# Transposed S5 input projection with a DRAM ring, and a background placed behind the residual, in a two-layer trunk

## The chip, the cores and the metric

One core of one Trainium2 chip runs the whole kernel. The metric is device time in microseconds of one execution. Matmuls run on TensorE (PE), elementwise work on VectorE (DVE), ScalarE (ACT) and GpSimd (POOL); transfers are issued from the queue of SyncE (SP) or, where the code says so, from GpSimd's.

## The reference

The program is a trunk of two layers on one sequence of 1024 positions and 1024 channels, in fp32. Each layer has a mixer and an MLP, and each of the four is wrapped as

```
shift, scale, gate = silu(c) @ W_mod + b_mod
x <- LayerNorm(alpha * x + (1 + gate) * sublayer(x * (1 + scale) + shift))
```

Layer 0's mixer is multi-head latent attention, layer 1's is S5, a diagonal state-space layer:

```
u = h @ w_in                                     # 1024 x 1024
bu = einsum(u in 64 groups of 16 channels, B)    # 64 complex states for each group
x_t = a * x_(t-1) + bu_t                         # a scan over the positions
y = Re(C x) + d * u
g = gelu(y);  z = g * sigmoid(g @ w_glu + b_glu);  return z @ w_out
```

The MLP is `relu(h @ w1 + b1)**2 @ w2 + b2` with 4096 hidden channels.

## The kernel before

Every large product is done on operands split in a high and a low part (`split`, L73 to L75: ACT copies the high part, DVE or POOL subtracts for the low one), with three matmuls for each (`mm3`, L78 to L80: high·high, high·low, low·high). X is held as eight row blocks of 128 positions by 1024 channels. `to_hT` (L863) transposes a pair of row blocks on PE (L874), scales and shifts them on ACT (L877) and splits them (L880, L881); the result h has channels in partitions and positions along the free axis, in two halves of 512 positions.

A scheduler sorts each engine's instructions by a simulation of the program, and each engine works its list off in that order; a semaphore wait at the head of a list holds everything behind it. `issue_after` adds an order without a wait between engines. So a text order in the code is a wish, and the list of each engine is what counts.

**MLP.** `mlp` runs 32 blocks of hidden channels, two per round g. `load1` loads and splits a block of w1, `load2` a block of w2 (L1005 multiplies it by the gate first), `mm1` makes the hidden block for one half of the positions into a PSUM tile of pool "a1" (two tiles) and squares it (ACT L1026 to L1028, DVE L1029), `mm2` multiplies by w2, and `accumulate` adds to X on DVE (L829). The residual (`alpha * x` with gain and bias) is done on X by POOL (L885, L886) before the first accumulation. `tick`, called in `mm1` and `mm2`, runs steps of a generator `bg` at a rate `pace`: in MLP 0 these are the modulations of three later sublayers (loads L561, products L563 on POOL and L568 on DVE, transposes L588) and the parameters of S5; in MLP 1 `bg` is empty.

**S5.** When MLP 0 closes, `finish0` normalises a row block, writes it to `x_d` and, after each second one, calls `to_hT`. The projection `u_strip(qr, s)` makes strip s (128 positions) of a quarter of the channels: positions are rows, 256 channels are columns, 24 matmuls, and ACT copies the PSUM tile to U (L1347). There are 32 such strips. The layer then runs 16 `front(b)`, each on four groups of channels: it transposes U by four PE transposes (L1385) with an ACT copy (L1388), applies B (L1392, 16 matmuls on the chip), rotates and scans on DVE (L1401 to L1406) and rotates back (L1409, one half on POOL, one on DVE) into zz. `back(b)` (L1417 to L1419, 24 matmuls) makes y, ACT applies the gelu (L1424), and every second back transposes it (L1432). A back follows its front by two. Tables of each front come in one load `pt` (1.5 MB, four buffers) and one `tz` for each pair.

**GLU.** For 8 blocks of channels and two halves of the positions a product lands in a PSUM tile of "a1" (L1472 on), the sigmoid and the gate follow, and `split` stores zT.

## Time and profile before

| | us |
|---|---|
| median of three runs | 2356.4 (2353.73 to 2360.72) |
| profiled execution, its own time | 2353.56 |
| its span, first to last instruction | 2351.4 |
| mean granted TensorE clock | 0.978 |
| MLP 0, from its first residual to its last matmul | about 485 to 1239 |
| S5, to the first GLU matmul | about 1239 to 1440 |
| MLP 1, with its end | about 1620 to 2351 |

A row of the waits reads: the engine and the line that waited, the engine and tile it waited for, then the sum in us, how often, and the longest. A row of the windows reads: the stretch, its length, then busy time and number of instructions of PE, PE's weight loads, DVE, ACT and POOL, then the granted clock, the busy share of the DMA engines and GB/s. A row of the timeline reads: start, duration, engine, line, operation, and in brackets the idle time before it with what ended it. Matmul records overlap by their pipelining, so the spacing of their starts is the cost of one.

### The profile page before, as it was taken

The numbers are of one execution on the slowest core, as the hardware profiler recorded it, in microseconds if no ns is written. First come the engines' busy times: TensorE is split into PE (matmuls) and PEld (weight loads), VectorE is DVE, ScalarE is ACT, GpSimd is POOL, SyncE is SP. The second block draws the span as 40 slices with busy tenths as digits, with TensorE's granted clock in tenths as the row PEclk, the third lists the DMA queues.
The fourth block names the chain that finished last, engine by engine and source line by source line (L and its number), as shares of the span: only waits on it lengthen the run. The fifth ranks groups of instructions, "written<-read, shape, count | busy, mean of one in ns | idle before, by whom it ended". The sixth has DMA issues, their size and how long they took to land.

```text
span 2351.4 us, 29181 instructions
## 1 busy us (share of the span) xinstructions
PE 2241.3 (95%) x11039; PEld 1885.4 (80%) x11039; DVE 1420.1 (60%) x2473; ACT 831.6 (35%) x1399; POOL 626.5 (27%) x731
## 2 busy tenths in 40 slices
PE   7799998979999999999998998999999999999996
PEld 6678886867788788888888997878788888888885
DVE  8877786387777766676444445454744444444437
ACT  3477774442222323333235233324322222222321
POOL 5534767371000334333021212433500000000005
PEclk8899998989999999999999999999999999999998
DMA  7222224135453345446123554330211111111201
GB/s 257 62 62 61 85 99 170 32 111 167 150 163 113 96 110 144 127 116 158 51 81 144 162 167 157 108 99 28 72 54 45 45 59 40 54 54 36 63 27 72
DMA packets 191579, 229.44 MB, mean 98 GB/s; under 512 B 45361, under 2 KB 136764, under 8 KB 189390
## 3 DMA queue, kind: packets, MB, share of 16 engines
q1 hardware_dynamic: 186558, 214.98, 29.4%
q0 software_dynamic: 3840, 12.59, 1.7%
q8 instruction: 87, 1.43, 0.2%
q14 instruction: 54, 0.44, 0.1%
q10 hardware_dynamic: 1040, 0.00, 0.0%
HBM read 190.88 MB, written 34.54 MB: 96 GB/s over the span
## 4 chain that ended last, share of the span: by engine, by line
PE 48%; DVE 3%; DMA 2%; ACT 1%; issue 1%; SPq 0%; POOL 0%; DVEq 0%; ACTq 0%; POOLq 0%
PE a L78 8%; PE a L80 8%; PE a L79 8%; PE mm L78 7%; PE mm L79 7%; PE mm L80 7%; PE mm L1392 1%; DMA wor<-in_ssm_w_out_dram 1%; DMA pt<-prm_d 1%; DVE ct L75 1%; PE a L1419 0%; PE a L1418 0%; PE a L1417 0%; DVE wo L75 0%; DVE X L1518 0%
## 5 line engine op out<-in xcount | busy, mean ns | idle before, releaser
L829 DVE TENSOR_TENSOR X<-X,mm 128x512 f32<-128x512 f32 x478 | 322.6, 684 | 286.1 <-PE mm L80 282.2
L78 PE MATMUL mm<-pb 128*128 128x512 f32 x512 | 203.0, 397 | 5.8 <-DVE X L829 5.8
L78 PE MATMUL a<-hT,pb 128*128 128x512 f32 x496 | 195.6, 394 | 11.0 <-DVE pb L1029 10.7
L79 PE MATMUL mm<-pb 128*128 128x512 f32 x512 | 199.7, 390 | 0.0
L80 PE MATMUL mm<-pb 128*128 128x512 f32 x512 | 199.7, 390 | 0.0
L80 PE MATMUL mm<-ct 128*128 128x512 f32 x512 | 199.2, 389 | 0.0
L79 PE MATMUL mm<-ct 128*128 128x512 f32 x512 | 199.2, 389 | 0.0
L78 PE MATMUL mm<-ct 128*128 128x512 f32 x512 | 198.5, 390 | 0.0
L78 PE MATMUL a<-hT,ct 128*128 128x512 f32 x496 | 193.3, 390 | 3.3 <-DVE ct L1029 3.3
L1026 ACT ACTIVATE a<-a,vt 128x512 f32<-128x512 f32 x128 | 83.5, 652 | 314.5 <-PE a L80 314.3
L80 PE MATMUL a<-hT,pb 128*128 128x512 f32 x496 | 194.4, 392 | 0.0
L79 PE MATMUL a<-hT,pb 128*128 128x512 f32 x496 | 194.4, 392 | 0.0
L80 PE MATMUL a<-hT,ct 128*128 128x512 f32 x496 | 193.1, 389 | 0.0
L79 PE MATMUL a<-hT,ct 128*128 128x512 f32 x496 | 193.0, 389 | 0.0
L885 POOL TENSOR_TENSOR X<-X,rb 128x1024 f32<-128x1024 f32 x6 | 14.8, 2480 | 634.5 <-ACT X L861 634.5
L1005 DVE TENSOR_TENSOR w2r<-w2r,gffn 128x1024 f32<-128x1024 f32 x64 | 87.6, 1371 | 132.4 <-DMA w2r<-in_mlp_w_dram 132.3
L78 PEld LDWEIGHTS a<-hT,pb 128*128 128x128 f32 x496 | 94.0, 190 | 31.7 <-DVE pb L1029 12.4
L78 PEld LDWEIGHTS mm<-pb 128*128 128x128 f32 x512 | 96.2, 188 | 27.3 <-DVE X L829 7.5
L78 PEld LDWEIGHTS mm<-ct 128*128 128x128 f32 x512 | 95.9, 188 | 20.9 <-DVE X L829 0.6
L80 PEld LDWEIGHTS mm<-pb 128*128 128x128 f32 x512 | 96.1, 188 | 20.2
L79 PEld LDWEIGHTS mm<-ct 128*128 128x128 f32 x512 | 96.2, 188 | 20.0
L79 PEld LDWEIGHTS mm<-pb 128*128 128x128 f32 x512 | 96.2, 188 | 19.7 <-issue 0.7
(492 smaller groups left out, 5414.5 us busy)
## 6 DMA issues: line engine op xcount, KB each, us to landing
w1r<-in_mlp_w_dram SPq DMA_DIRECT2D x64, 512.0 KB, 4.1
w2r<-in_mlp_w_dram SPq DMA_DIRECT2D x64, 512.0 KB, 3.3
pt<-prm_d SPq DMA_DIRECT2D x16, 1536.0 KB, 7.2
mb<-in_mod_mix_w_dram SPq DMA_DIRECT2D x41, 256.0 KB, 2.6
prm_d<-cb SPq DMA_DIRECT2D x80, 128.0 KB, 2.4
wm<-in_mod_mix_w_dram SPq DMA_DIRECT2D x8, 1024.0 KB, 11.8
mb<-in_mod_ffn_w_dram POOLq DMA_DIRECT2D x32, 256.0 KB, 3.0
mb<-in_mod_ffn_w_dram SPq DMA_DIRECT2D x32, 256.0 KB, 3.0
```

Source lines behind the costliest of these rows:

```text
L75: (eng or V).tensor_tensor(lo, src, f32(hi), ALU.subtract)
L78: PE.matmul(ps, lh, rh, start=start, stop=False)
L79: PE.matmul(ps, lh, rl, start=False, stop=False)
L80: PE.matmul(ps, ll, rh, start=False, stop=stop)
L829: V.tensor_tensor(xh, xh, ps[h], ALU.add)
L885: P.tensor_tensor(X[t], X[t], ra, ALU.mult)
L1005: V.tensor_tensor(r, r, gate, ALU.mult)
L1026: S.activation(ps, ps, AF.Relu, bias=vt2[:, l * 32 + j:l * 32 + j + 1])
L1392: PE.matmul(pvv[i][:, g * 128:g * 128 + 128], pt[:, i, g], ug[:, g], start=True, stop=True)
```

## The change

1. **Projection, transposed.** For layer 1 `to_hT` stores the strips in reversed order (`rev`). `u_half(m, hf)` now makes 128 channels by 512 positions: the weights are stationary, h is moving, 24 matmuls with 512 columns, 16 halves. ACT copies a half into U (L1357). When both halves of a channel block m are there, SP writes the block to DRAM (`ud[m]`, 512 KB, L1359), and `ug_load(b)` reads it back as four groups by 16 channels × 8 strips in partitions, with four transfers of 64 KB on GpSimd's queue (L1364), into a ring of four entries in the free part of U. `ug_load(b + 2)` stands behind `front(b)` and the back of b − 2. The transposes of U and their copies go.
2. **Loads of the projection's weights** come as 8 of 512 KB, one for each m, instead of 16 of 256 KB.
3. **Background.** `tick` does nothing until g = 1; then every step is ordered behind the load of w1 for that round. `pace` of MLP 0 goes from 0.6 to 0.66.
4. **Residual** in halves of 512 channels: four POOL operations for each row block.
5. **GLU**: the second half of each block takes its PSUM tile from pool "mm" (four tiles).

The order on DVE at the start of MLP 0, where the first squared hidden blocks (L1029 before, L1039 now; pb<-a) and the first weights are made. Before:

```order
L1029 TENSOR_TENSOR pb<-a_5174,pb 128x512
L881 TENSOR_TENSOR hT<-mm,hT 128x2x256 x4
L1005 TENSOR_TENSOR w2r<-w2r,gffn 128x1024 x2
L75 TENSOR_TENSOR pb<-w2r,pb 128x1024 x2
L568 SCALAR_TENSOR_TENSOR mb<-mb,csT 128x512
L1216 MEMSET tC 128x16
L1005 TENSOR_TENSOR w2r<-w2r,gffn 128x1024
L1217 MEMSET tC 128x16
L568 SCALAR_TENSOR_TENSOR mb<-mb,csT 128x512 x2
L75 TENSOR_TENSOR pb<-w2r,pb 128x1024
L1029 TENSOR_TENSOR pb<-a_5207,pb 128x512
L568 SCALAR_TENSOR_TENSOR mb<-mb,csT 128x512
```

Now:

```order
L1039 TENSOR_TENSOR pb<-a_5145,pb 128x512
L884 TENSOR_TENSOR hT<-mm,hT 128x2x256 x4
L1011 TENSOR_TENSOR w2r<-w2r,gffn 128x1024 x2
L1039 TENSOR_TENSOR pb<-a_5174,pb 128x512
L75 TENSOR_TENSOR pb<-w2r,pb 128x1024
L1227 MEMSET tC 128x16
L1228 MEMSET tC 128x16
L75 TENSOR_TENSOR pb<-w2r,pb 128x1024
L1039 TENSOR_TENSOR pb<-a_5203,pb 128x512
L1011 TENSOR_TENSOR w2r<-w2r,gffn 128x1024
L75 TENSOR_TENSOR pb<-w1r,pb 128x1024
L829 TENSOR_TENSOR X<-X,mm 128x512
```

The products of the background (L568) are gone from this stretch; the first of them stands nine rows further on. The hidden block that stood behind the third w2 product (L1005) now stands ahead of it.

On PE in the tail of S5, behind the last projection matmul. L1392 (now L1405) is a front, L1417 to L1419 (now L1430 to L1432) a back, each back with its own PSUM tile a. Before, around the last but one front:

```order
L1419 MATMUL a_12639<-pt,zz 128x128
L1392 MATMUL mm<-pt 128x128 x8
L1417 MATMUL a_12712<-tz,pt 128x128
L1418 MATMUL a_12685<-pt,zz 128x128
L1419 MATMUL a_12685<-pt,zz 128x128
```

Now, around the same front:

```order
L1405 MATMUL mm<-U,pt 128x128 x8
L1430 MATMUL a_12141<-tz,U 128x128
L1430 MATMUL a_12205<-tz,U 128x128
L1431 MATMUL a_12141<-pt,zz 128x128
L1405 MATMUL mm<-U,pt 128x128 x8
L1432 MATMUL a_12141<-pt,zz 128x128
```

Before, the back of b = 12 (a_12639 in the first row) was complete when front 14 came, and fronts 12 and 13 with two backs stood between back 10 and it. Now front 14 (the second row of L1405) follows front 13 with only three back matmuls between them, and backs 11 to 14 stand behind it.

On POOL in the tail of S5, where the first half of each zz is made (L1408 and L1409, now L1421 and L1422). Before:

```order
L1409 TENSOR_TENSOR zz<-pt 128x4x127
L1408 MEMSET zz 128x4
L1409 TENSOR_TENSOR zz<-pt 128x4x127 x2
L1408 MEMSET zz 128x4
L1462 TENSOR_SCALAR r_12778<-r_12778 128x512
L1409 TENSOR_TENSOR zz<-pt 128x4x127
```

Now:

```order
L1364 DMA U<-ud_5046 128x1x128 x4
L1421 MEMSET zz 128x4 x2
L1364 DMA U<-ud_5046 128x1x128
L1422 TENSOR_TENSOR zz<-pt 128x4x127 x3
L1364 DMA U<-ud_5046 128x1x128 x3
L1422 TENSOR_TENSOR zz<-pt 128x4x127
```

The loads of the ring (L1364, here those of the last channel block, for fronts 14 and 15) now stand between the zz rows, as they do throughout S5; each waits for the back that frees its place in the ring, and the zz rows behind it on POOL wait with it.

The diff, whole:

```diff
--- before.py
+++ after.py
@@ -860,12 +860,15 @@
         E.tensor_scalar(nm, mu, rs, -1.0, ALU.mult, ALU.mult)
         S.activation(X[t], X[t], AF.Identity, bias=nm, scale=rs)
 
-    def to_hT(ts, n, A, tile=None):
+    def to_hT(ts, n, A, tile=None, rev=False):
 
         g = len(ts)
         m = 4 // g
-        hi, lo = A[ts[0] // 4]
-        c0 = (ts[0] % 4) * 128
+        p0 = ts[0]
+        if rev:
+            p0, ts = 7 - ts[-1], ts[::-1]
+        hi, lo = A[p0 // 4]
+        c0 = (p0 % 4) * 128
         for k0 in range(0, 8, m):
             ps = (tile or tr_tile)()
             for k in range(m):
@@ -882,8 +885,10 @@
         return last_.ins
 
     def residual(t, ra, rb):
-        P.tensor_tensor(X[t], X[t], ra, ALU.mult)
-        P.tensor_tensor(X[t], X[t], rb, ALU.add)
+        for r, op in ((ra, ALU.mult), (rb, ALU.add)):
+            for h in range(2):
+                sl = slice(h * 512, h * 512 + 512)
+                P.tensor_tensor(X[t][:, sl], X[t][:, sl], r[:, sl], op)
 
     def res_row(wp, v, al=ALPHA, gb2=None, name="rb"):
 
@@ -994,8 +999,9 @@
             if j >= NJ:
                 return
             r = wp.tile([128, 8, 128], F32, tag="wr", name="w1r")
-            SY.dma_start(r, w1r[j])
+            d = SY.dma_start(r, w1r[j])
             split(*w1_buf(j), r)
+            return d.ins
 
         def load2(j):
             if j >= NJ:
@@ -1007,11 +1013,15 @@
             return d.ins
 
         credit = [0.0]
+        behind = []
 
         def tick(w):
+            if not behind:
+                return
             credit[0] += w * pace
             while credit[0] >= 1.0:
-                step(bg)
+                with tc.issue_after(behind[0]):
+                    step(bg)
                 credit[0] -= 1.0
 
         def mm1(j, h):
@@ -1061,8 +1071,9 @@
             residual(t, ra, rb)
         for g in range(NJ // 2 - 2):
             j = 2 * g + 2
-            load1(j + 1)
+            d = load1(j + 1)
             if g:
+                behind.append(d)
                 mm1(j, 0)
             mm1(j, 1)
             load2(j)
@@ -1325,26 +1336,32 @@
 
     gTf = []
     kdr = kd.rearrange("g a f -> a g f")
-    wir = ssm_w_in[0].rearrange("(k p) f -> p k f", p=128)
+    wir = ssm_w_in[0].rearrange("(k p) (m f) -> m p k f", p=128, f=128)
+    ud = [drm.tile([128, 1024], F32, name=f"ud{m}") for m in range(8)]
     WI = {}
 
-    def u_load(qr):
-
-        WI[qr] = [xp.tile([128, 2, 2, 256], F32R, tag="X", name="wi") for _ in range(4)]
-        for i in range(4):
-            if i % 2 == 0:
-                r2 = wp.tile([128, 2, 2, 256], F32, name="wir", **(dict(tag="a4", bufs=1) if qr else dict(tag="wr")))
-            r = r2[:, i % 2]
-            SY.dma_start(r, wir[:, 2 * i:2 * i + 2, qr * 256:qr * 256 + 256])
-            split(WI[qr][i][:, :, 0], WI[qr][i][:, :, 1], r, V if qr else P)
-
-    def u_strip(qr, s):
-        ps = a1_tile()[:, 0:256]
+    def u_load(m):
+
+        r = wp.tile([128, 8, 128], F32, name="wir", **(dict(tag="wr") if m < 2 else dict(tag="a4", bufs=1)))
+        SY.dma_start(r, wir[m])
+        WI[m] = [xp.tile([128, 8, 128], F32R, tag="X", name="wi") for _ in range(2)]
+        split(*WI[m], r, P if m < 2 else V)
+
+    def u_half(m, hf):
+
+        ps = a1_tile() if hf and m < 3 else mm_half()
+        wh, wl = WI[m]
+        hh, hl = T5["h"][hf]
         for k in range(8):
-            hh, hl = [q[:, k, (s % 4) * 128:(s % 4) * 128 + 128] for q in T5["h"][s // 4]]
-            w_ = WI[qr][k // 2]
-            mm3(ps, hh, hl, w_[:, k % 2, 0], w_[:, k % 2, 1], k == 0, k == 7)
-        S.activation(U[:, qr % 2, :, 7 - s], ps.rearrange("p (g c) -> p g c", g=16), AF.Copy)
+            mm3(ps, wh[:, k], wl[:, k], hh[:, k], hl[:, k], k == 0, k == 7)
+        S.activation(U[:, m % 2, hf * 512:hf * 512 + 512], ps, AF.Copy)
+        if hf == 0:
+            SY.dma_start(ud[m], U[:, m % 2])
+
+    def ug_load(b):
+        us = ud[b // 2].rearrange("(g c) (s n) -> g s c n", c=16, s=8)
+        for g in range(4):
+            P.dma_start(UG[b % 4][:, g], us[(4 * b + g) % 8])
 
     def finish0(t, ps):
         accumulate(t, ps)
@@ -1355,17 +1372,19 @@
         norm(t)
         SY.dma_start(x_d[t], X[t])
         if t % 2:
-            to_hT((t - 1, t), 1, T5["h"], mm_half if t == 7 else None)
+            to_hT((t - 1, t), 1, T5["h"], mm_half if t == 7 else None, True)
         if t == 5:
             u_load(0)
-
-    mixer = mlp(0, hT, cont, gffn, wp, bg, finish0, w1x, rb, pace=0.6)
+            u_load(1)
+
+    mixer = mlp(0, hT, cont, gffn, wp, bg, finish0, w1x, rb, pace=0.66)
     next(mixer)
     mixer.send(o_end(7, ps))
     step(mixer, 100)
 
 
-    U = pa1.tile([128, 2, 16, 8, GC], F32, tag="pa", name="U")
+    U = pa1.tile([128, 4, 1024], F32, tag="pa", name="U")
+    UG = [U[:, 2 + i // 2, (i % 2) * 512:(i % 2) * 512 + 512].rearrange("p (g n) -> p g n", g=4) for i in range(4)]
     tzG = {}
 
     BK = {}
@@ -1379,13 +1398,7 @@
                 SY.dma_start(tz[16 * s:16 * s + 16], kdr[:, 4 * b:4 * b + 8, 16 * s:16 * s + 128])
             tzG[0] = tz
             tzG[1] = {}
-        ps = tr_tile()
-        for g in range(4):
-            gl = (4 * b + g) % 16
-            PE.transpose(ps[:, g * 128:g * 128 + 128],
-                         U[:, (b // 4) % 2, gl].rearrange("p s c -> p (s c)"), ident)
-        ug, w = pt[:, 6], pt[:, 7]
-        S.activation(ug.rearrange("p g n -> p (g n)"), ps, AF.Copy)
+        ug, w = UG[b % 4], pt[:, 7]
         pvv = mm_tile()
         for i in range(2):
             for g in range(4):
@@ -1432,19 +1445,23 @@
                     PE.transpose(ps[:, i * 128:i * 128 + 128], G[:, 4 * h + i], ident)
                 S.activation(gTf[k][:, h * 512:h * 512 + 512], ps, AF.Copy)
 
-    for s in range(8):
-        u_strip(0, s)
-    strips = {0: (1, 0, 2), 1: (1, 2, 4), 2: (1, 4, 6), 3: (1, 6, 8), 5: (2, 0, 2), 6: (2, 2, 5), 7: (2, 5, 8),
-              9: (3, 0, 2), 10: (3, 2, 5), 11: (3, 5, 8)}
+    u_load(2)
+    for hf in (1, 0):
+        for m in range(2):
+            u_half(m, hf)
+    for b in range(4):
+        ug_load(b)
     for b in range(16):
-        if b in (0, 3, 7):
-            u_load((0, 3, 7).index(b) + 1)
-        qr, s0, s1 = strips.get(b, (0, 0, 0))
-        for s in range(s0, s1):
-            u_strip(qr, s)
+        m = b // 2 + 2
+        if m < 8:
+            if b % 2 == 0 and m > 2:
+                u_load(m)
+            u_half(m, 1 - b % 2)
         front(b)
         while len(BK) > 2:
             back(min(BK))
+        if 2 <= b < 14:
+            ug_load(b + 2)
     while BK:
         back(min(BK))
     q = pa_tiles([128, 4, 1024], F32R, "gT")
@@ -1469,7 +1486,7 @@
         split(gh, gl, r)
         for hf in range(2):
             sl = slice(hf * 512, hf * 512 + 512)
-            ps = a1_tile()
+            ps = a1_tile() if hf == 0 else mm_half()
             for k in range(8):
                 mm3(ps, gh[:, k], gl[:, k], gTh[k][:, sl], gTl[k][:, sl], k == 0, k == 7)
             S.activation(ps, ps, AF.Sigmoid, bias=vt1[:, VGLU + m:VGLU + m + 1])
```

## Prediction

> **What bounds the kernel now.** I read the page first, the busy time of the engines.
>
> ```profile
> PE 2241.3 (95%) x11039; PEld 1885.4 (80%) x11039; DVE 1420.1 (60%) x2473; ACT 831.6 (35%) x1399; POOL 626.5 (27%) x731
> ```
>
> TensorE (PE) is busy 2241.3 of the span's 2351.4 us, so an edit can pay in two ways only: less work on PE, or less of its 110 us of idle time (and of the slow clock that follows idle time). So the second view is what PE waited for:
>
> ```profile
> PE a L78 <- DVE pb L1029: 10.7, 1, 10.7
> PE mm L78 <- DVE X L829: 7.5, 7, 1.9
> PE tr L874 <- DVE h L881: 4.2, 3, 1.7
> PE a L78 <- ACT U L1347: 3.5, 1, 3.5
> PE a L78 <- DVE zT L75: 3.4, 1, 3.4
> ```
>
> The longest single wait of the kernel stands first: 10.7 us at the start of MLP 0. The others lie at the entry of the S5 layer (L874, L1347) and at the first GLU tiles (zT); L829's seven are spread over both MLPs. The third view is stretches around the longest wait (busy time of PE, its weight loads, DVE, ACT and POOL; then the granted clock), the fourth the timeline of VectorE (DVE) there:
>
> ```profile
> 490.00:500.00 10.00, 7.71 (x32) 5.99 (x32) 8.54 (x10) 8.31 (x17) 10.00 (x5) 0.74 0.27 80
> ...
> 520.00:525.00 5.00, 0.00 (x0) 0.00 (x0) 4.98 (x2) 1.48 (x3) 5.00 (x3) 0.50 0.34 105
> 525.00:530.00 5.00, 3.33 (x8) 2.66 (x9) 5.00 (x4) 0.00 (x0) 5.00 (x2) 0.50 0.53 160
> 530.00:535.00 5.00, 5.00 (x19) 3.98 (x18) 5.00 (x4) 0.14 (x1) 4.36 (x2) 0.77 0.59 207
> ...
> sum 50.00, PE 36.99 PEld 29.53 DVE 46.28 ACT 18.68 POOL 44.36; mean PE 4.62 PEld 3.69 DVE 5.79 ACT 2.34 POOL 5.55
> ```
>
> ```profile
> 517.17 2.81 DVE L568 SCALAR_TENSOR_TENSOR mb<-mb,csT 128x512 f32<-128x512 f32 x1
> 522.66 3.35 DVE L75 TENSOR_TENSOR pb<-w2r,pb 128x1024 fp32r<-128x1024 f32 x1
> 525.94 0.68 DVE L1029 TENSOR_TENSOR pb<-a,pb 128x512 fp32r<-128x512 f32 x1
> 537.22 0.74 DVE L568 SCALAR_TENSOR_TENSOR mb<-mb,csT 128x512 f32<-128x512 f32 x1
> 539.68 1.22 DVE L75 TENSOR_TENSOR pb<-w1r,pb 128x1024 fp32r<-128x1024 f32 x1
> ```
>
> From 490 to 540 us PE idles 13.0 us (50.00 less 36.99), with the clock down to 0.50. DVE is full: background products (L568) and weight splits (L75) stand ahead of the L1029 that PE waits for, and while GpSimd (POOL) is full with the residual they take 2.81 and 3.35 us instead of 0.74 and 1.22.
>
> **Term A, entry of MLP 0: −12.** What is lost there now: 13.0 idle; the longest wait on L829, 1.9, which comes just after; and the busy time at a low clock, 7.71 × 0.26 + 3.33 × 0.50 + 5.00 × 0.23 = 4.8. Together 19.7 us. The change moves the background (its products, transposes and loads) behind g=1, so no L568 is left ahead of the first splits, and cuts each residual into halves. What stays can be read off MLP 1, the same code with an empty background:
>
> ```profile
> 700.00:730.00 30.00, 30.00 (x138) 24.95 (x137) 23.73 (x34) 9.40 (x13) 0.70 (x1) 1.00 0.55 176
> 1620.00:1650.00 30.00, 27.89 (x136) 22.99 (x135) 12.46 (x26) 19.97 (x37) 17.72 (x9) 0.97 0.15 53
> 1650.00:1680.00 30.00, 26.65 (x110) 20.73 (x109) 26.60 (x16) 11.09 (x16) 28.13 (x10) 0.97 0.26 88
> ```
>
> Idle 2.1 + 3.4, clock loss 60 × 0.03 = 1.8: 7.3 us. 19.7 − 7.3 = 12.4; I take 12, since one L563 that waits for a load still stands between the last residual halves. Bounds −8 (the 10.7 alone, of which one stretched operation, 2.8, stays) to −17 (nearly all of it). The background itself is not dearer: in 700–730 PE is full with DVE at 23.7 of 30, and its last transposes come 97 matmuls (22 us) later in PE's order, still ahead of the S5 layer. If that cover were gone, its 124 steps would end up on the S5 entry.
>
> **Term B, S5 work on PE: −12.2.**
>
> ```profile
> L78 PE MATMUL a<-wi,h 128*128 128x256 f32 x244 | 70.5, 290 | 3.5 <-ACT U L1347 3.5
> L1385 PE MATMUL tr<-ident,U 128*128 128x128 f32 x64 | 9.3, 273 | 0.0
> L1409 POOL TENSOR_TENSOR zz<-pt 128x508 f32<-128x508 f32 x16 | 27.3, 1704 | 137.6 <-DVE zz L1408 126.8 <-PE tr L1432 10.8
> ```
>
> Matmul records overlap, so I price by starts: 256 columns 0.12 us apart, 512 columns 0.226 apart:
>
> ```profile
> 1240.14 0.28 PE L78 MATMUL a<-wi,h 128*128 128x256 f32 x1
> 1240.26 0.28 PE L79 MATMUL a<-wi,h 128*128 128x256 f32 x1
> ...
> 1236.39 0.39 PE L78 MATMUL mm<-pb 128*128 128x512 f32 x1
> 1236.62 0.39 PE L79 MATMUL mm<-pb 128*128 128x512 f32 x1
> ```
>
> 768 × 0.12 = 92.2 becomes 384 × 0.2265 = 87.0: −5.2. The 64 transposes of U (L1385), 0.11 apart, go: −7.0. ScalarE's 16 copies after them go too; it has room. Bounds ±1.
>
> **Term C, S5 entry: +3 (−3 to +8).**
>
> ```profile
> 1250.00:1255.00 5.00, 2.04 (x16) 1.63 (x15) 2.68 (x4) 5.00 (x12) 0.07 (x1) 1.00 0.10 29
> 1255.00:1260.00 5.00, 1.38 (x7) 1.17 (x8) 3.28 (x6) 4.96 (x12) 0.00 (x0) 0.60 0.93 355
> ...
> L877 ACT ACTIVATE tr<-tr,bcol,acol 128x256 f32<-128x256 f32 x16 | 8.3, 568 | 5.2 <-PE tr L874 4.0 <-DVE bni L122 1.3
> L880 ACT ACTIVATE h<-tr 128x512 fp32r<-128x512 f32 x8 | 5.0, 656 | 0.0
> ```
>
> ScalarE's chain (scale, split of h) is full here and PE starves: 6.6 us. That chain keeps its length. But before, projection matmuls fill the gaps ahead of the last X transposes (26 of them, 3.1 us); in the changed order the transposes come first. In ScalarE's changed order 22 scalings (0.57), 9 splits (0.66) and two weight splits (about 1) stand between the last row block of X and the first copy of U: 20.5 us, so it comes near 1265. By then PE has done 46 wide matmuls (10.4 us) instead of some 120 narrow ones (14.4): 4 us behind. I take 3, as nothing later in the entry waits for ScalarE's U copies of a single strip (the 3.5 of L1347) any more. First front: after its half, 34 matmuls (7.7 us) stand ahead of it on PE; the trip takes 0.6 copy, 3.1 write, 0.6 issue, 2.9 load = 7.2, so it is just covered.
>
> ```profile
> x_d<-X SPq DMA_DIRECT2D x8, 512.0 KB, 3.1
> ...
> L561 POOL DMA_DIRECT2D mb<-in_mod_ffn_w_dram x32: 538/587/587, 142.6 to 309.5; - x32
> ...
> DMA to landing us min/median/max: 2.5/2.9/5.3
> ```
>
> In the steady part each front gets 4 GpSimd issues: 4 × 0.57 + 1.7 (its zz) = 4.0 us of about 10.4 per front (half 5.4, front 1.8, back 2.7, transposes 0.4). On POOL some zz stand behind an issue that waits for the back two fronts before; PE then has another back and transposes (3.8 us) in hand. Nothing to 0.5 each; in C's range.
>
> **Term D, S5 tail: +4 (0 to +10).** pt has four buffers, so pt(14) loads only when back(10) is done.
>
> ```profile
> 1400.69 1.79 PE mm L1392 x16
> 1409.06 12.61 DMA pt<-prm_d
> 1430.51 1.80 PE mm L1392 x16
> 1437.43 0.49 PE a L1419 x2
> ...
> pt<-prm_d SPq DMA_DIRECT2D x16, 1536.0 KB, 7.2
> ```
>
> Before, the last projection ends at T0 = 1400.5, pt(14) starts 8.5 us later, takes 12.6 (two at once), and front(14) follows at once; GLU begins at T0 + 39. Now PE does after T0 front(11) (1.8), eight transposes (0.9), front(12) (1.8) and back(10) (24 × 0.11 = 2.7): pt(14) can start at T0 + 7.2 and lands 7.2 later, or more. Front(14) follows right behind front(13), at T0 + 9.5: a stall of 5. The backs put behind it cover pt(15) but leave front(15) to its own chain of scans: 5.1 us (1430.51 + 1.8 to 1437.43). The tail ends near T0 + 38.5, though it holds 4.9 us less work (back(9), transposes); 2.7 of that was only moved before T0. So about 4 of B's gain is not seen.
>
> **Terms E, F, G.** E: the 3.4 us at zT comes of having two PSUM tiles for all sigmoid halves, so that the third half waits until the first is read out; now every second half takes a tile of another pool: −3.4 (−4 to 0, should that pool's tiles be held by the S5 tail). F: halves in MLP 1: −1 (−3 to +1). G, at the end:
>
> ```profile
> 2330.20 4.71 DVE L1518 SCALAR_TENSOR_TENSOR X<-X,bmv,rb 128x512 f32<-128x512 f32 x2
> 2342.70 1.40 DVE L1519 SCALAR_TENSOR_TENSOR X<-X,bny,rb 128x512 f32<-128x512 f32 x2
> ```
>
> The same form takes 2.36 beside POOL and 0.70 alone; halves let it in earlier: −2 (−4 to 0).
>
> **Sum.** −12 − 12.2 + 3 + 4 − 3.4 − 1 − 2 = −23.6, from the profiled execution's 2353.6 to 2330.0. The median shown is 2.8 above that execution, so I forecast 2332 for a median.
>
> **Rivals.** (1) The S5 gain goes to its seams: C at +8 and D at +10 cost 11 more: 2344. For it: two starved chains are touched; against: the ring looks ahead two fronts. (2) The MLP 0 wait was DVE beside POOL, not the background: splits still take 3.35, A is −4: 2341. For it: L75 is stretched without L568; against: MLP 1. (3) Slower: GpSimd's queue becomes the bound. Issues for b+4 wait for back(b), and a zz stands behind them, so back(b), 4 issues, zz and the next back form a loop: 4d + 1.7 + 2.7 against 10.4 per front. It binds from d = 1.5 us. If DVE stretches an issue as it is stretched itself (2.81/0.74 = 3.8, so d = 2.17), 13 fronts lose 2.7 each: 35 more, 2367; the whole gain is eaten from d = 2. Against it: the 32 issues in the attention part took 538 to 587 ns. (4) The change does not do what it says: the background returns in a burst behind g=1 and stalls L829 there, A −2: 2343.
>
> On rival 3, the Trainium skill, "SBUF — State Buffer" (A bandwidth-pool intuition that's wrong), states that a GpSimd-queued DMA of about 620 ns takes about 3100 ns beside a DVE copy, as its descriptors wait for the port. By that rule the loop would be 16.8 us, an estimate of 83 us lost in 13 fronts, and the kernel near 2415; no row here shows such an issue, and the 587 ns speak against it.
>
> **Chances.** Forecast 0.60, rival 1 0.18, rival 2 0.10, rival 3 0.07, rival 4 0.05. Range: the forecast's terms reach 2318 with A at −17 and the seams at their best halves; above, it takes in rivals 1, 2 and 4 to 2350. 0.3% (7 us) is what a measurement can tell from no change. The forecast and most of rivals 1, 2 and 4 are below 2349: faster 0.83; their upper ends same 0.09; rival 3 and mishaps of the seams slower 0.08.
>
> **What would show it.** A: no wait above 3 us on the L1039 that was L1029, and a clock near 1 in 510–540. B: no transposes of U, 384 matmuls 0.226 apart. C: PE waits between the last MLP matmul and the first front of 8 to 14 us in sum. D: one wait on pt for front(14), one on zz after front(15). E: no wait on zT. Rival 3: issues of L1364 above 1.5 us and PE waiting on zz in every front. The forecast is wrong if the S5 layer as a whole is not shorter, or if MLP 0's entry still loses over 13 us.

## The result and the profile after

The changed kernel takes 2382.6 us (median of 4 runs, 2378.8 to 2387.8) against 2356.8 for the kernel before: a ratio of 1.011 (95% interval 1.0084 to 1.0136). It is slower by 26 us where 24 us faster was forecast. The profiled execution took 2384.7 us, its span is 2383.0.

Where the time went, by the starts of the first and last matmuls of each stage in the two traces (us; the differences, each rounded by itself, add up to the difference of the spans, 31.6, within 0.1):

| stretch | before | after | difference |
|---|---|---|---|
| up to the first hidden block of MLP 0 (pb in L78) | 480.2 | 482.3 | +2.1 |
| from there to the last matmul of MLP 0 | 759.4 | 742.3 | −17.1 |
| S5 and GLU, to the last matmul of the GLU | 292.3 | 313.3 | +21.0 |
| output projection, to the first hidden block of MLP 1 | 93.1 | 93.7 | +0.7 |
| from there to MLP 1's first product with w2 | 29.7 | 49.9 | +20.2 |
| the rest of MLP 1 | 678.8 | 676.4 | −2.3 |
| from its last matmul to the end | 18.1 | 25.0 | +6.9 |

So the entry of MLP 0 gave more than was forecast, and three other places lost 48 us. The page of the changed kernel shows nearly the same busy time of TensorE, with 448 instructions fewer (64 transposes and 384 matmuls), over a longer span; the waits of TensorE show the new places:

```profile
PE 2242.5 (94%) x10591; PEld 1869.8 (78%) x10591; DVE 1416.1 (59%) x2467; ACT 819.7 (34%) x1359; POOL 666.3 (28%) x837
```

```profile
PE mm L78 <- ACT ct L74: 20.2, 1, 20.2
PE mm L1405 <- DMA pt<-prm_d: 11.4, 4, 3.9
...
PE mm L1405 <- DMA U<-ud: 5.1, 2, 4.5
PE tr L877 <- DVE h L884: 4.1, 1, 4.1
...
PE a L78 <- DVE pb L1039: 2.9, 3, 1.9
```

The 10.7 us on pb (L1029, now L1039) are down to 2.9 in three waits. On top stands a wait of 20.2 us that did not exist, in MLP 1, where the kernel's own code changed by nothing but the halves of the residual. The next two rows are S5's: fronts that wait for their tables (pt) and for the ring (ud).

**Entry of MLP 0.** The stretch in which TensorE was busy for 19.27 us of 30, before and after:

```profile
510.00:540.00 30.00, 19.27 (x74) 15.36 (x73) 27.74 (x21) 7.01 (x10) 24.36 (x9) 0.77 0.46 149
510.00:540.00 30.00, 27.98 (x116) 22.31 (x114) 19.14 (x19) 6.99 (x11) 27.66 (x19) 0.94 0.37 115
```

**Entry of MLP 1.** Before, the first two multiplications of w2 by the gate (L1005, now L1011) took 5.88 us beside whole residuals:

```profile
1650.94 5.88 DVE L1005 TENSOR_TENSOR w2r<-w2r,gffn 128x1024 f32<-128x1024 f32 x2
```

Now, in the timelines of VectorE, ScalarE, GpSimd and TensorE:

```profile
1657.65 23.91 DVE L1011 TENSOR_TENSOR w2r<-w2r,gffn 128x1024 f32<-128x1024 f32 x2
1681.48 0.68 DVE L1039 TENSOR_TENSOR ct<-a,ct 128x512 fp32r<-128x512 f32 x1
...
1680.46 2.19 ACT L74 ACTIVATE ct<-w2r 128x1024 fp32r<-128x1024 f32 x2 [23.07 <-DVE w2r L1011]
...
1654.78 11.16 POOL L891 TENSOR_TENSOR X<-X,rb 128x512 f32<-128x512 f32 x9
...
1674.40 4.94 POOL L891 TENSOR_TENSOR X<-X,rb 128x512 f32<-128x512 f32 x4
...
1681.57 2.07 PE L78 MATMUL mm<-ct 128*128 128x512 f32 x4 [20.18 <-ACT ct L74]
...
L1011 DVE TENSOR_TENSOR w2r<-w2r,gffn x4: 1211/1226/22776, 1657.7 to 1699.0; 128x1024 f32<-128x1024 f32 x4
```

The same two multiplications take 23.91 us; the last row (shortest, median and longest of the line's operations) tells that one of them took 22.8 us where the median is 1.2. It begins at 1657.7 and ends just after GpSimd's row of halves does: the row ends at 1674.40 + 4.94 = 1679.3, the operation at 1680.4, about its own length of 1.2 us later. GpSimd's halves meanwhile run through at 1.24 us each, as if alone. ScalarE waits for the product, TensorE for ScalarE. In MLP 0 of the same execution the same pair of operations beside the same halves took 3.94 us, and the halves gave way:

```profile
498.37 3.94 DVE L1011 TENSOR_TENSOR w2r<-w2r,gffn 128x1024 f32<-128x1024 f32 x2
...
487.72 17.97 POOL L891 TENSOR_TENSOR X<-X,ra 128x512 f32<-128x512 f32 x12
```

**The end.** The same once more, with the last layer norm's residual:

```profile
2354.80 13.41 DVE L1535 SCALAR_TENSOR_TENSOR X<-X,bmv,rb 128x512 f32<-128x512 f32 x2
...
2337.18 29.82 POOL L891 TENSOR_TENSOR X<-X,rb 128x512 f32<-128x512 f32 x24 [657.84 <-ACT X L861]
```

13.41 us for two operations that took 4.71 before; they end a little after GpSimd's 24 halves do (2367.0).

**S5.** TensorE's waits in its timeline, and what the loads cost:

```profile
1229.95 1.97 PE L877 MATMUL tr<-ident,X 128*128 128x128 f32 x8 [4.08 <-DVE h L884]
1276.32 1.22 PE L1405 MATMUL mm<-U,pt 128*128 128x128 f32 x4 [4.45 <-DMA U<-ud]
1315.38 0.98 PE L1405 MATMUL mm<-U,pt 128*128 128x128 f32 x3 [3.87 <-DMA pt<-prm_d]
1343.84 0.87 PE L1405 MATMUL mm<-U,pt 128*128 128x128 f32 x5 [2.83 <-DMA pt<-prm_d]
1389.18 0.57 PE L1405 MATMUL mm<-U,pt 128*128 128x128 f32 x3 [2.04 <-DMA pt<-prm_d]
1411.78 0.46 PE L1405 MATMUL mm<-U,pt 128*128 128x128 f32 x2 [2.62 <-DMA pt<-prm_d]
...
L1364 POOL DMA_DIRECT2D U<-ud x64: 582/622/762, 1272.9 to 1425.5; - x64
DMA to landing us min/median/max: 2.2/3.9/9.8
```

The issues on GpSimd are short (at most 0.76 us), so they are not stretched. Their landing takes 3.9 us in the median and up to 9.8. Three of the waits on pt lie ahead of the last projection matmul (1401), where before TensorE waited for nothing from the first front on, and two of them lie in stretches with a lower granted clock:

```profile
1310.00:1340.00 30.00, 26.13 (x163) 23.88 (x162) 12.26 (x23) 5.58 (x10) 11.32 (x17) 0.89 0.66 193
1340.00:1370.00 30.00, 27.17 (x157) 23.99 (x157) 14.47 (x29) 4.46 (x8) 8.32 (x14) 0.94 0.96 258
```

Cut at the same events, S5 before and after: from MLP 0's last matmul to the first front 48.8 and 51.7 us; from there to the last projection matmul 112.1 and 124.9; from there to the last transposes of the gelu 41.0 and 47.1. None of the 12.2 us of work that went is seen in these lengths. The rows of the whole stretch from MLP 0's last matmul to the GLU's, before and after, show what covers it:

```profile
1239.57:1531.83 292.26, 276.77 (x1969) 258.12 (x1968) 133.61 (x231) 104.76 (x182) 70.91 (x66) 0.98 0.44 146
1224.60:1537.90 313.30, 281.37 (x1530) 244.45 (x1528) 135.68 (x227) 96.15 (x150) 113.63 (x132) 0.93 0.53 163
```

TensorE's idle time grew from 15.5 to 31.9 us, and its clock went down: it stood at 0.50 for 10.2 us before and for 44.4 after, in nine pieces of 3.4 or 6.8 us. Five of these pieces begin within, or less than 1 us behind, a wait of 2.6 to 4.5 us in the timeline above. Multiplying busy time by the missing share of the clock, as the prediction did for MLP 0, but cut at each change of the clock, gives a loss of 3.5 us before and 19.0 after. What is left of the busy time, the work at full clock, is 273.3 and 262.3 us. By this estimate 11 us of work did go, and 16 us of new waits together with 16 us of slow clock hide it.

### The profile page after: what moved, and what is told of

The parts are those of the page before. It is cut to its first block, busy times and chain, and to the rows that moved or that the text cites. A ratio compares the mean times of both kernels' runs of the same rounds, so it can differ in the third digit from the quotient of the medians.

```text
span 2383.0 us, 28399 instructions
## 1 busy us (share of the span) xinstructions
PE 2242.5 (94%) x10591; PEld 1869.8 (78%) x10591; DVE 1416.1 (59%) x2467; ACT 819.7 (34%) x1359; POOL 666.3 (28%) x837
## 3 DMA queue, kind: packets, MB, share of 16 engines
q1 hardware_dynamic: 191678, 219.18, 29.7%
## 4 chain that ended last, share of the span: by engine, by line
PE 66%; DVE 6%; DMA 5%; POOL 3%; issue 2%; ACT 1%; SPq 1%; DVEq 0%; POOLq 0%; ACTq 0%
PE mm L78 12%; PE mm L80 12%; PE mm L79 12%; PE a L78 9%; PE a L80 9%; PE a L79 9%; POOL X L891 2%; DVE w2r L1011 1%; DMA pt<-prm_d 1%; DMA w2r<-in_mlp_w_dram 1%; PE mm L1405 1%; DVE X L1535 1%; DVE X L829 1%; DMA wor<-in_ssm_w_out_dram 1%; PE tr L877 0%
## 5 line engine op out<-in xcount | busy, mean ns | idle before, releaser
L891 POOL TENSOR_TENSOR X<-X,rb 128x512 f32<-128x512 f32 x56 | 75.1, 1386 | 657.8 <-ACT X L861 657.8
L78 PE MATMUL mm<-ct 128*128 128x512 f32 x512 | 199.2, 391 | 20.2 <-ACT ct L74 20.2
L78 PE MATMUL mm<-pb 128*128 128x512 f32 x512 | 201.9, 396 | 3.7 <-DVE X L829 3.5
L78 PE MATMUL a<-hT,pb 128*128 128x512 f32 x496 | 195.9, 395 | 2.9 <-DVE pb L1039 2.9
L78 PE MATMUL a<-hT,ct 128*128 128x512 f32 x496 | 193.5, 390 | 0.0
L1011 DVE TENSOR_TENSOR w2r<-w2r,gffn 128x1024 f32<-128x1024 f32 x64 | 105.5, 1651 | 133.1 <-DMA w2r<-in_mlp_w_dram 133.0
L78 PEld LDWEIGHTS mm<-ct 128*128 128x128 f32 x512 | 96.5, 189 | 40.7 <-ACT ct L74 20.6
L78 PEld LDWEIGHTS mm<-pb 128*128 128x128 f32 x512 | 96.4, 188 | 26.2 <-DVE X L829 5.4
L78 PEld LDWEIGHTS a<-hT,pb 128*128 128x128 f32 x496 | 93.6, 189 | 23.9 <-DVE pb L1039 4.2
L80 PEld LDWEIGHTS mm<-pb 128*128 128x128 f32 x512 | 96.4, 188 | 20.3
```

Source lines behind the costliest of these rows:

```text
L78: PE.matmul(ps, lh, rh, start=start, stop=False)
L80: PE.matmul(ps, ll, rh, start=False, stop=stop)
L891: P.tensor_tensor(X[t][:, sl], X[t][:, sl], r[:, sl], op)
L1011: V.tensor_tensor(r, r, gate, ALU.mult)
```

## The experiments

The executions of these kernels spread by some us (the kernel before lay between 2350 and 2377 over all the comparisons below), so sizes of a few us are read from traces, and the medians serve for what is larger.

### The parts alone

First each part by itself, or left out. The halves alone (`h_only`) put these lines in the kernel before:

```diff
-        P.tensor_tensor(X[t], X[t], ra, ALU.mult)
-        P.tensor_tensor(X[t], X[t], rb, ALU.add)
+        for r, op in ((ra, ALU.mult), (rb, ALU.add)):
+            for h in range(2):
+                sl = slice(h * 512, h * 512 + 512)
+                P.tensor_tensor(X[t][:, sl], X[t][:, sl], r[:, sl], op)
```

> The kernel before with one part of the change: the residual in halves (MLP 0, MLP 1 and the last layer norm). Theory A: a row of POOL halves of 512 keeps VectorE's two-input operations out until the row ends; the wait of 20 us at the start of MLP 1 and the longer end (25 us from the last matmul instead of 18) come of this alone: 2356 + 20 + 7 = about 2383, with one VectorE multiplication of w2 of over 15 us near 1650. Rival B: those waits come of the other parts (what runs where in MLP 1 is shifted by 7 us): then within 2 us of before, and no VectorE operation over 4 us there.

Measured: 2378.9 us (9 runs, 2359.6 to 2390.0) against 2357.3, ratio 1.0094 (1.0066 to 1.0123). Two runs lie at 2360, seven from 2372.6 up. The profiled one was of the two, and its timeline of VectorE shows the entry of MLP 1 undisturbed, the end not:

```profile
1653.36 4.53 DVE L1007 TENSOR_TENSOR w2r<-w2r,gffn 128x1024 f32<-128x1024 f32 x2
...
2331.60 13.42 DVE L1520 SCALAR_TENSOR_TENSOR X<-X,bmv,rb 128x512 f32<-128x512 f32 x2
```

The end lasted 24.3 us here instead of 18.1. So the halves alone cost about 20 us in most executions; theory A holds in size, but not in every execution, as its wording implied.

The changed kernel with whole residuals (`no_h`, the diff above reversed):

> The changed kernel with the residual whole again. Theory A: the 20 us at the start of MLP 1 and the 7 us at the end go, 2382.6 - 27 = about 2355, no better than before, as the S5 layer and the GLU still lose what MLP 0 gains. If halves were what helped the entry of MLP 0, 10 of its 17 us go as well: about 2365. Rival B: 2380 or more.

Measured: 2366.8 us (6 runs, 2360.7 to 2379.0), ratio 1.0053 (1.0023 to 1.0082): 16 us less than the changed kernel, and still slower than before. Theory A's 2355 was missed by the median. In the trace, which is of the fastest run, both waits are gone: 29.6 us to MLP 1's first product with w2, and 18.0 at the end. MLP 0 is 12.6 us shorter than before there instead of 17.1, so the halves give some 4 us in MLP 0, not 10. Other traces agree in size: in the first 100 us behind MLP 0's first hidden block TensorE idles 8.0 to 8.3 us in three with the background behind and whole residuals (`no_h`, `b_only`, `bg`), and 4.0 to 6.1 in three with halves there (the changed kernel, `bgh0`, `full`).

The background part alone (`b_only`):

```diff
+        behind = []
         def tick(w):
+            if not behind:
+                return
             credit[0] += w * pace
             while credit[0] >= 1.0:
-                step(bg)
+                with tc.issue_after(behind[0]):
+                    step(bg)
...
-    mixer = mlp(0, hT, cont, gffn, wp, bg, finish0, w1x, rb, pace=0.6)
+    mixer = mlp(0, hT, cont, gffn, wp, bg, finish0, w1x, rb, pace=0.66)
```

> The kernel before with one part of the change: the background of MLP 0 behind the residual (and the pace 0.66). Theory C: the background's products ahead of the splits were the 10.7 us; MLP 0 ends 12 to 17 us earlier and nothing gives it back: 2340 to 2345. Rival D: the entry got better because the POOL halves let VectorE in sooner; with whole residuals VectorE stays stretched (2.8 to 3.4 us an operation) and only 4 us are won: about 2352.

Measured: 2347.9 us (10 runs, 2343.0 to 2354.2), ratio 0.9955 (0.9941 to 0.9969). The median lies between the two forecasts, so the trace has to decide. In it MLP 0 is 13.6 us shorter; nothing after it differs by more than 2 us. Its operations on VectorE are as stretched as before (up to 3.4 us beside whole residuals), so theory C holds and D falls: what was ahead in the queue counted, not how long each operation took. The size varies from trace to trace: with the same background, MLP 0 is only 7.2 us shorter than before in `bg`'s.

The transposed projection alone (`s_only`, parts 1 and 2 of the change without the rest):

> The kernel before with one part of the change: the transposed projection with its ring (reversed strips, loads on GpSimd's queue); residual, background and GLU as before. Theory E: the S5 layer from the last matmul of MLP 0 to the last transpose of the gelu takes 224 us instead of 202, whatever comes before it: 2356 + 22 = about 2378. Rival F: the S5 layer was longer only because the later background and the earlier entry collided with it; then the 12 us less work on TensorE show, 2344 to 2350.

Measured: 2378.4 us (4 runs, 2374.4 to 2382.6), ratio 1.0097 (1.0082 to 1.0112). Theory E holds: the S5 part costs 21 us by itself, before any other part touches it, and S5 takes the 224 us forecast. F falls.

### Halves: where, and how often

In the last layer norm alone (`h_end`) and in MLP 1 alone (`h_mlp1`), by a flag for `residual`:

```diff
-    def residual(t, ra, rb):
-        P.tensor_tensor(X[t], X[t], ra, ALU.mult)
-        P.tensor_tensor(X[t], X[t], rb, ALU.add)
+    def residual(t, ra, rb, halves=False):
+        n = 512 if halves else 1024
+        for r, op in ((ra, ALU.mult), (rb, ALU.add)):
+            for c in range(0, 1024, n):
+                sl = slice(c, c + n)
+                P.tensor_tensor(X[t][:, sl], X[t][:, sl], r[:, sl], op)
```

> Residual halves in MLP 1 alone. Theory A: whether VectorE's first multiplication of w2 is kept out there is a matter of chance from one execution to the next; runs of two kinds, about 2356 and about 2376, with nothing between that is not the spread of the kernel before. Rival: the two kinds belong to the end or to MLP 0; then all runs within 3 us of before.

Measured: 2375.8 us, ratio 1.0067 (1.0047 to 1.0086). One run of twelve took 2352.9, eleven lie between 2371.0 and 2383.8, and none between. The profiled one is of the eleven (2383.8):

```profile
1661.42 25.29 DVE L1008 TENSOR_TENSOR w2r<-w2r,gffn 128x1024 f32<-128x1024 f32 x2
1686.63 0.68 DVE L1032 TENSOR_TENSOR ct<-a,ct 128x512 fp32r<-128x512 f32 x1
```

25.3 us for the two operations, up to the end of GpSimd's row of halves (1684.5). Only this execution of the twelve has a trace, but two traces of kernels with halves everywhere, of executions that took 2361 and 2357 us (`h_only` above, `h_dep` below), show no such operation in MLP 1. So whether it is kept out there changes from one execution to the next, here 11 to 1 against it, at a price of about 20 us.

> Residual halves in the last layer norm alone. In every profile with halves one VectorE operation at the end was kept out for 12.8 us while the POOL halves ran through, in none with whole ones. Theory A: +6 to +7 us in every run, with little spread: 2356 + 6.5 = about 2363. If the 20 us of the slow executions came of the end too, the runs spread up to 2385.

Measured: 2359.0 us (12 runs, 2352.2 to 2378.3), ratio 1.0004 (0.9978 to 1.0030): the expectation was missed. In its trace the operations at the end took turns with the halves, and the end lasted 18.0 us as before:

```profile
2331.79 3.50 DVE L1521 SCALAR_TENSOR_TENSOR X<-X,bmv,rb 128x512 f32<-128x512 f32 x2
```

In three traces with halves everywhere (the changed kernel, `h_only`, `h_dep`) one operation at the end was kept out for 12.8 us; here none was. So the 7 us at the end of the changed kernel are not the price of halves in every case. Whether chance decides there too, or what runs ahead of it, one trace can't tell, and 7 us do not stand out of a spread of 26.

The halves alone, written half by half (`h_dep`):

```diff
-        for r, op in ((ra, ALU.mult), (rb, ALU.add)):
-            for h in range(2):
-                sl = slice(h * 512, h * 512 + 512)
+        for h in range(2):
+            sl = slice(h * 512, h * 512 + 512)
+            for r, op in ((ra, ALU.mult), (rb, ALU.add)):
```

> The residual in halves alone, but written half by half: product and sum of the first half, then of the second, so that at the end of the program each POOL instruction needs the one just before it. If a row of independent POOL halves keeps VectorE out because one follows the other without a gap, the end takes 18 to 19 us from the last matmul, not 24, and the runs lie 5 to 7 us lower than with halves alone. If the length of the instruction decides, the end stays at 24 us and the runs spread from 2360 to 2390 as with halves alone.

Measured: 2376.9 us (12 runs; two at 2355 and 2357, ten from 2371 to 2382), ratio 1.0060 (1.0036 to 1.0084). The trace, of the run at 2357, has an operation of 12.8 us at the end as with halves alone. At the start of MLP 1 GpSimd's list was the same as with halves alone, so only the end tests this, and product and sum cannot be told apart there in the trace. A need of one half for the one before does not let VectorE in, as far as this shows. Why whole operations gave way in every profile and halves often don't stays open.

### What holds S5 up

The writes of u from ScalarE's queue instead of SyncE's (`s_act`), the other parts of the change left out as in `s_only`:

```diff
-            SY.dma_start(ud[m], U[:, m % 2])
+            S.dma_start(ud[m], U[:, m % 2])
```

> The transposed projection alone, as before, but the writes of u to DRAM are issued from ScalarE's queue, right behind the copy that fills U, instead of SyncE's. Theory G: on SyncE's queue these writes wait 57 us in sum for ScalarE's copies, and the loads of the tables (pt, tz) stand behind them; freed of that, TensorE's waits on pt and tz (about 11 us, and 5 or more of slow clock after them) go: 2378 - 12 to 18 = 2360 to 2366. Rival H: the tables come late because the ring's traffic shares the DMA engines with them; then 2374 or more, with the same waits on pt.

Measured: 2377.0 us (6 runs, 2372.2 to 2385.0), ratio 1.0071 (1.0046 to 1.0096). No change against `s_only`; theory G falls. TensorE's waits on the ring and on the tables, first of `s_only`, then of `s_act`, have nearly the same sum, 16.7 and 15.2:

```profile
PE mm L1397 <- DMA pt<-prm_d: 8.9, 3, 4.0
PE mm L1397 <- DMA U<-ud: 7.8, 3, 4.5
```

```profile
PE mm L1397 <- DMA U<-ud: 8.5, 3, 4.6
PE mm L1397 <- DMA pt<-prm_d: 6.7, 3, 3.2
```

The ring loads from SyncE's queue instead of GpSimd's (`s_sp`):

```diff
-            P.dma_start(UG[b % 4][:, g], us[(4 * b + g) % 8])
+            SY.dma_start(UG[b % 4][:, g], us[(4 * b + g) % 8])
```

> The transposed projection alone, but the 64 ring loads are issued from SyncE's queue instead of GpSimd's. Theory G: SyncE's queue is what stalls, and 64 more issues that wait for backs make it worse: 2383 to 2398. Rival 3 of the prediction (GpSimd's queue with zz behind it is the cost): 2370 or less.

Measured: 2368.1 us (10 runs, 2362.7 to 2372.7), ratio 1.0033 (1.0015 to 1.0051): 10 us less than `s_only`, against theory G and for the prediction's rival 3, though not by its mechanism. In the traces, from the last matmul of MLP 0 to the last of the GLU, 311.5 us became 304.7 (292.3 before the change). GpSimd's waits in the changed kernel show what the loads do on its queue:

```profile
POOL U L1364 <- PE mm L1405: 31.0, 3, 17.5
POOL U L1364 <- DMA ud<-U: 30.1, 1, 30.1
POOL zz L1422 <- DVE zz L1421: 25.7, 8, 7.7
POOL U L1364 <- PE a L1430: 24.3, 6, 8.9
```

The ring loads wait for fronts and backs to free their place, 55 us in sum, and the zz rows stand behind them. Four of the 16 zz products (at 1310, 1335, 1366 and 1416) begin right behind a load without a wait of their own, two of them 3.6 and 4.9 us after VectorE's scan that they need. With the loads on SyncE this is gone: all 16 begin as their input comes. That it was worth the 7 us is not shown: in the changed kernel TensorE waited 0.3 us in all for a zz of GpSimd's. Of the 6.8 us between the two traces, by the estimate used for S5 above, about 2 are idle time of TensorE and about 6 its slow clock (17.6 us lost became 11.5), while the work came out 1.6 longer. And since the scheduler sorted every list anew, the gain is that of the queue and of the new order together.

Both moves at once (`s_sa`):

> The transposed projection alone, with the writes of u on ScalarE's queue and the ring loads on SyncE's. With the ring loads alone moved to SyncE it took 2368, with the writes alone moved 2377. If SyncE's queue still holds the tables up by the writes (24 us of waits there), 2368 - 3 to 6 = 2362 to 2365. If the order of fronts and backs decides, about 2368.

Measured: 2372.7 us (4 runs, 2363.1 to 2378.5), ratio 1.0057 (1.0036 to 1.0079); by the trace S5 and GLU take 304.5 us, as in `s_sp`. The place of the writes makes no difference that can be seen.

The load of the tables cut in three, the first-needed part first (`s_pt3`, on top of `s_sp`):

```diff
-        SY.dma_start(pt[:, 0:6].rearrange("p a b c -> p a (b c)"), prm_d[b])
+        for i in (0, 4, 2):
+            SY.dma_start(pt[:, i:i + 2].rearrange("p a b c -> p a (b c)"), prm_d[b][:, i:i + 2])
```

> The transposed projection alone with the ring loads on SyncE (2368), and each front's table load cut in three of 512 KB: the two tables that TensorE reads first come first. Theory J: fronts wait for tables because backs come in bunches of two or three, so that two or three loads of 1.5 MB run at once; with the first third landing early the waits on pt at fronts (about 10 us here) go, with the slow clock behind them: 2352 to 2360. Rival K: the fronts only wait for something else then (the ring, tz, zz): 2366 to 2370.

Measured: 2362.3 us (10 runs, 2354.5 to 2370.0) beside a before of 2361.0, ratio 1.0002 (0.9980 to 1.0023): 6 us less than `s_sp`, 2 us above theory J's range. TensorE's waits in S5, first of `s_sp`, then of `s_pt3`:

```profile
PE mm L1397 <- DMA pt<-prm_d: 11.1, 6, 6.1
PE mm L1397 <- DMA U<-ud: 4.1, 1, 4.1
PE tr L877 <- DVE h L884: 4.1, 1, 4.1
```

```profile
PE a L1423 <- DMA U<-ud: 4.1, 1, 4.1
PE tr L877 <- DVE h L884: 4.1, 1, 4.1
PE mm L1398 <- DMA U<-ud: 3.4, 1, 3.4
```

The waits on pt are gone from the top of the list, and from the first front to the last projection matmul the trace takes 110.3 us instead of 115.0 in `s_sp`, 124.0 in `s_only` and 112.1 before the change. TensorE waits for nothing in this stretch, at a mean clock of 0.97. S5 and GLU together take 296.8 us: still 4.5 more than before. The first front comes 47.0 us after MLP 0, 1.8 earlier than before; the loss lies behind the last projection matmul, where 48.6 us stand against 41.0. The wait of a back on the ring (4.1 us) is there, and more slow clock.

The first projection weights two row blocks earlier as well (`s_all`):

```diff
+        if t == 3:
+            u_load(0)
         if t == 5:
-            u_load(0)
             u_load(1)
```

> As the last one, and the first projection weights loaded two row blocks earlier. If the entry of S5 loses its 6 us because the split of these weights comes late on ScalarE, 3 to 5 us less than the last one; if the transposes of X and their scalings hold the entry, the same within 2 us.

Measured: 2364.5 us (10 runs, 2355.1 to 2366.0), ratio 1.0013 (1.0000 to 1.0026). No gain: the wait of 4.1 us of the X transposes for VectorE's splits (L884) stays, and it comes ahead of every projection matmul; the first front comes after 46.9 us instead of 47.0. That these weights came late is not what holds the entry. The stretch of fronts and projection, 110.3 us in `s_pt3`, takes 114.3 in this trace, so a gain of 2 us over the 112.1 of before is within what two traces differ by.

### Better than both

The background behind, with the second GLU halves in the other pool (`bg`):

```diff
-            ps = a1_tile()
+            ps = a1_tile() if hf == 0 else mm_half()
```

> The background behind the residual and the second GLU halves in the other PSUM pool, nothing else of the change. The wait of 3.4 us on zT goes without a new one: 2347.9 (background alone) - 3 = about 2345. If the pool is held by something else there: 2348.

Measured: 2342.0 us (8 runs, 2332.5 to 2357.5), ratio 0.9915 (0.9882 to 0.9948). The wait on zT (3.4 us in `b_only` too) is not in its trace, and no new one stands in the GLU, which from the last transposes of the gelu on takes 86.1 us instead of 90.4 before.

With halves in the residual of MLP 0 alone (`bgh0`, by the flag above with `l == 0`):

> The background behind the residual, the second GLU halves in the other pool, and halves in the residual of MLP 0 alone. In MLP 0 the halves shorten VectorE's waits from 2.8 to 3.4 us an operation to 1.7 to 2.3 (changed kernel's profile), worth 3 us there: 2342 - 3 = about 2339. If the halves keep VectorE out there too in some executions, runs of 2355 and more appear.

Measured: 2335.9 us (4 runs, 2328.7 to 2338.0), ratio 0.9900 (0.9883 to 0.9916). This is the lowest median of all, 22 us under the kernel before, though its interval and `bg`'s overlap. The entry of MLP 0 in it:

```profile
510.00:540.00 30.00, 25.93 (x112) 20.31 (x111) 17.95 (x24) 5.64 (x8) 19.98 (x15) 1.00 0.49 153
```

The same with the mended S5 part (`full`):

> Background behind the residual, halves in MLP 0 alone, second GLU halves in the other pool, and the transposed projection with ring loads on SyncE, cut table loads and early weights. Against the same without the transposed projection (2335.9). Theory J makes S5 as long as before or up to 5 us shorter: 2331 to 2337. Rival K: 2345 or more.

Measured: 2344.8 us (5 runs, 2330.5 to 2376.0), ratio 0.9915 (0.9887 to 0.9942). One of the five lies 31 us above the next. By these times it can't be told from `bgh0`. By the traces S5 and GLU take 295.8 us in it and 286.1 in `bgh0`; 5.0 of the 9.7 us lie between the last projection matmul and the last transposes of the gelu, and 3.5 in the GLU. Rival K comes nearer: even mended, the transposed projection does not pay here.

## Why the prediction was wrong

The prediction summed to −23.6 on the profiled execution's scale; +31.6 came. By its own steps:

- **Term A (entry of MLP 0, −12) was right**, by what it said would go: TensorE's idle time in MLP 0 fell from 20.3 to 7.0 us, its loss by the slow clock from 6.2 to 3.4. MLP 0 came out 13.6 us shorter with the background alone (7.2 in `bg`'s trace) and 17.1 with the halves. Rival 2 is out, as the stretched operations stayed in `b_only` and the gain came all the same.
- **Terms F and G (halves, −1 and −2) had the wrong sign.** The step that failed is "halves let it in earlier". It took for granted that two engines that slow each other take turns, so that a shorter operation of the one means a shorter wait of the other. They did take turns in every profile with whole operations, and with halves in MLP 0. In MLP 1 and at the end one VectorE operation was kept out for all that was left of the row of halves: 22.8 and 12.8 us. `h_only` (+21.7 by medians) and `h_mlp1` (+18.3) show that the halves alone do it. This is about half of the miss. The bound of "+1" came from no row; the before trace had none for such halves beside VectorE.
- **Terms B, C and D (S5, −5.2 in sum) came out as +21.** Term B was right: by the estimate above 11 us of work went, 12.2 were forecast. The step that failed most is the sentence on the steady part, "nothing to 0.5 each". It priced POOL's own time (four issues and a zz in a front) and its own chain, and forgot the table loads: from the first front to the last projection matmul TensorE, which waited for nothing before, waited 8.7 us, all for tables. And the slow clock behind waits, which term A counted, was put at nothing in B, C and D without a reason: 14 us more of it came up to the last transposes of the gelu, by the same estimate.
- **How the tables came late.** For the front at 1343.8 they were issued at 1334.4, just as a back ended, and TensorE waited 2.8 us for them; before, the same load was issued 14.3 us ahead of its front. The loads are not slower (7.7 us in the median and 9.9 at most, against 7.2 and 12.6). Backs now end in bunches (at 1334.3, 1337.0 and 1340.6, after 23.7 us without one), so the loads that wait for them start late. It is argued, not shown, that zz rows held up by ring loads made these bunches: `s_sp` has bunches too, with no zz held up. `s_sp` (−7 by the trace, −10 by medians) and `s_pt3` (another −8 by the trace) together give back 15 of 19 us; the rest lies in the tail.
- **Term C (+3) had the number by luck.** The first front came 2.9 us later against MLP 0's end, but it waited 4.5 us for the ring, whose trip was said to be "just covered" by the 34 matmuls ahead of it. Idle time grew by 3.5 us there and the loss by the clock by 3.8; less work made up for the rest.
- **Term D** was 45 instead of 38.5 us from the last projection matmul to the end of the last back. The waits that it named were smaller than forecast (2.6 us on pt and 2.5 on zz, where about 5 each was forecast), but others stood beside them (2.1 on tz, 1.1 on the gate's weights), and 5.9 us went to the slow clock instead of 1.7 before.
- **Rival 3 had the place and not the mechanism.** Taking the loads off GpSimd's queue gave 7 to 10 us, but the issues took 0.58 to 0.76 us, not 2.2. What the loads did there was wait for their place, with zz behind them. The 3100 ns that the Trainium skill's page "SBUF — State Buffer" (A bandwidth-pool intuition that's wrong) gives for such a load beside a VectorE copy do not appear in any of the 64 issues; beside them VectorE ran products, sums, differences and scans in S5, no copy, so the rule itself was not tried.
- **Rival 1 named the seams and was too small** (11 us of loss; about 26 against the forecast of this part), since it kept to the entry and the tail and had no slow clock in it.
- **Term E** held in `bg`, where the GLU is 4.3 us shorter without the wait on zT. In the changed kernel it is 0.9 us shorter: 2.8 us of waits on the gate's weights stand there instead.

The prediction's own sign, that the forecast is wrong if the S5 layer as a whole is not shorter, came in. The chances were wrong too: 0.08 for slower, though the change had two parts whose worst rows had no like in the trace of before.

## What to carry to other kernels

Price an operation that another engine was seen to slow by whether it gets in at all, not by its own length: cutting GpSimd's work in smaller pieces beside VectorE is to be tried on the chip, stage by stage, and in several executions. Try a load that waits for its buffer on a queue where no compute stands behind it (here 7 to 10 us, with a new order of all lists), and when buffers are freed in bunches, cut the load so that what is read first lands first (here 6 to 8 us). Price a wait of TensorE with the slow clock that comes with it: in S5 and the GLU, 16 us of new waits came with 16 us more of it. When a change has several parts, time them apart: here one gave 10 us, and two cost 20 each.

## What the runs showed of the hardware

A single VectorE operation with two SBUF inputs was kept out for 22.8, 24.2 and 12.8 us by a row of GpSimd operations of 128x512 that ran at their own speed of 1.24 us. Beside GpSimd operations of 128x1024 no such VectorE operation took more than 3.4 us in any profile here. With halves both happened at the same place: in the trace of `h_mlp1` the operation at MLP 1's entry was kept out, in that of `h_only` it was not, and eleven executions of `h_mlp1` out of twelve were about 20 us longer than the twelfth. What decides it was not found. How far a GpSimd half had got when VectorE's operation came does not decide it alone: where the operation was kept out (five times) it came 0.09 to 0.40 us after the start of a half, and the multiplications of w2 got in after 0.17 us in MLP 0 of the changed kernel and after 0.29 us in MLP 1 of `h_dep`, in 2.2 and 2.1 us.

The Trainium skill, "SBUF — State Buffer" (SBUF: two separate sides), states that the pair of ports is an exclusive lock, held for one whole instruction, and that the loser blocks. The rows of 1.7 to 3.4 us agree with one instruction's wait; the 22.8 us do not, as 17 GpSimd instructions began and ended in them.
